# A streaming encoder layer: first normalisation in three steps, its transposed tiles through HBM by token tiles, and a right operand in four tiles

## Chip, cores and metric

The kernel runs on one core of a Trainium2 chip. Its matmuls run on TensorE (PE, whose weight loads PEld overlap them), elementwise work on VectorE (DVE), ScalarE (ACT) and GpSimd (POOL), and its DMAs are issued by SyncE (SP). The metric is the device time of one execution in microseconds (us), smaller is better; the median of three runs is given with their lowest and highest.

## What is computed

One layer over 2048 tokens of width 1024. The part before the output projection gives y (pooling and chunked attention over one input projection); what the change touches comes behind it:

```python
y = jnp.einsum('bse,ed->bsd', jnp.concatenate([y_pool, y_attn], axis=-1), w_out[l])
x = layer_norm(ALPHA * x + (1.0 + g1) * y, ln1_g[l], ln1_b[l])
h = x * (1.0 + sc2) + sh2
f = jnp.square(jax.nn.relu(jnp.einsum('bsd,df->bsf', h, w_ff1[l])))     # d_ff = 4096
f = jnp.einsum('bsf,fd->bsd', f, w_ff2[l])
x = layer_norm(ALPHA * x + (1.0 + g2) * f, ln2_g[l], ln2_b[l])
```

Inputs and output are float32. The kernel keeps that precision by cutting each operand into a rounded high part and a low remainder; a product is then three matmuls (high by high, high by low, low by high). Cutting (`split`) is a copy on ACT that rounds (CAST, L58) and a subtraction on DVE (L59).

## The kernel before

The program is one straight list of instructions for each engine, in the order in which the code is written; each engine takes its own list in order and waits on semaphores.

**Stages.** Attention and input projection run to about 640 us. Then comes the output projection with the first normalisation, to 873.8 us. FF1 follows to about 1532 us, and FF2 with the second normalisation ends the kernel.

**Output projection.** The 2048 tokens are 16 tiles of 128, t = 0 to 15. For each tile `st.get(yi[t])` gives the left operand: y is loaded from HBM (`raw<-yS`, L73) and cut into `hl`. The right operand, the weight `w_out`, cut, stands in one SBUF tile `hT` of 64 KB a partition. Each tile has two halves n of 24 matmuls (`wout_half`, L382), each into one of three PSUM banks `d`. `residual(t, n)` (DVE, L835) adds the bank to the tile of x, `xt`, and so frees it. After both halves `ln1_head` takes the statistics (DVE L773 and L775, three small POOL instructions) and writes the normalised tile `n` (ACT, L779). Tiles 0 to 2 are computed while the attention ends; the loop that matters runs over t = 3 to 15.

**From a normalised tile to FF1's operand.** `ln1_tail(u)` transposes a normalised tile u (8 PE transposes, L799, into one of two double-width PSUM tiles, T and S), scales it on ACT (8 instructions, L802) into `h`, and goes on by where the tile stands. Write b for the token half (tiles 0 to 7 and 8 to 15) and r = u mod 8. FF1 multiplies by seven combinations of quarter blocks (a Strassen scheme, pieces i = 0 to 6). For r < 4 two of the pieces are h itself. For r of 4 or more the tile's partner r − 4 comes back from HBM (`hp<-hS`, L796, two DMAs) and four DVE subtractions (`sums`, L820 to L823) make the other five. Pieces 0, 1, 2, 5 of token half 0 are cut into SBUF slots `sa` at once; the rest goes to HBM (`hS<-...`, L812). The tail of tile u stands between the two `residual` calls of a later tile t (u = t − 3 up to t = 6, where a second tail fits in, then u = t − 2). The last two tails come after the loop's body and behind the first products of FF1.

**FF1.** 32 groups g of output columns, seven products s each of 12 matmuls (L960): `f<-h,hl`, piece by weight combination. Results leave PSUM through an ACT copy `c` (L967) and DVE additions into tiles `g` (L973), are put through relu and square on ACT (L982, L983), combined, and stored (`fS<-g`, L1001). Pieces 3, 4 and 6 of token half 0 are loaded from `hS` in FF1's first group and cut there. The next group's weight is loaded, combined (`w_sums`, stored as `wS`) and cut (`w_split`) while a group runs.

**Order around the change.** All DMAs go through SP's one queue in program order. What a DMA waits for holds back all behind it. The buffers are few: two for `xt`, two for `raw`, three for `hl`, three for `n`, one each for `h` and `hp`.

Of the kernel before, what the change touches and what calls it, by code (L numbers as in the profile page):

```python
# [24 lines left out]
def trunk_layer(ctx: ExitStack, tc: tile.TileContext, xT, x, wada1, wada2, vecs, rows, win, wfirst, wpT, wout,  # L25
# [13 lines left out]
    hS = [[dram.tile([128, 4, 512], F32, name=f"hS{b}{i}") for i in range(7)] for b in range(2)]  # L39
# [74 lines left out]
    late = {}  # L114
    yi = [st.add(yS[t // 8][t % 8].rearrange("p k c -> p (k c)"), nc.vector) for t in range(16)]
    bigp = tc.tile_pool(name="big", bufs=1, side="right")
    big = bigp.__enter__()
    hT = big.tile([128, 2, 8, 1024], F32R, name="hT", tag="big")
# [42 lines left out]
    def dense0(k):  # L161
        for i, (a, b) in enumerate(((0, 0), (1, 0), (0, 1))):
            for c in range(NF0):
                for tb in range(2):
                    nc.tensor.matmul(first[c, tb], wf[:, a, k, c, :], hT[:, b, k, tb * 512:tb * 512 + 512],
                                     start=(k == 0 and i == 0), stop=(k == 7 and i == 2))
# [14 lines left out]
    def fold0(k):  # L181
# [6 lines left out]
        nc.scalar.activation(hT[:, 0, k, :], xk, AF.Identity, bias=mod1[:, k, 0:1], scale=mod1[:, k, 1:2])  # L188
        nc.scalar.activation(xk, xk, AF.Identity, bias=mod1[:, k, 0:1], scale=mod1[:, k, 1:2])

    def low0(k):
        wr, wa, xk = ld[k]
        nc.vector.tensor_sub(hT[:, 1, k, :], xk, hT[:, 0, k, :].bitcast(F32))
# [59 lines left out]
    def h_pieces(tb):  # L253
# [10 lines left out]
        for k in range(10):  # L264
# [131 lines left out]
    def dense():  # L396
        w, open_, side = {}, [], iter(())
        for hf, name, tb in blocks():
# [264 lines left out]
    def wo_pieces(n):  # L663
# [78 lines left out]
    def slot(i, name):  # L742

        pool, tag, n = (sap, "sa", 4) if i in (0, 1, 2, 5) else (late["sbp"], "sb", 3)
        return pool.tile([128, 2, 4, 512], F32R, name=name, tag=tag, bufs=n)

    cpool = tc.tile_pool(name="cp", bufs=1)
    cp = cpool.__enter__()
    lnp = tc.tile_pool(name="ln", bufs=1)
# [39 lines left out]
    def ln1_tail(t):  # L789
        b, r = t // 8, t % 8  # L790
        cols = slice((r % 4) * 128, (r % 4) * 128 + 128)
# [5 lines left out]
        pt = wide("S" if t % 2 and t < 15 else "T")  # L797
# [560 lines left out]
```

## Time and profile before

| what | value |
|---|---|
| median of 3 runs (lowest, highest) | 2167.26 us (2165.09, 2168.88) |
| the profiled execution: time, span of its trace | 2166.34 us, 2164.6 us |
| PE busy | 2059.5 us, 95% of the span |
| DVE, ACT, POOL busy | 61%, 46%, 20% |
| mean granted TensorE clock | 0.983 |
| output projection loop and FF1's first 18 products, 689.02 to 941.90 us | PE busy 222.80 of 252.88 us, clock 0.93 |
| FF1's middle, 1000 to 1500 us | PE busy 493.07 of 500 us, clock 0.99 |

The profiled execution was 1.74 us longer than its span, and 0.92 us under the median. A row of the trace gives the start, the busy time, the engine, the line of the code, the operation with its tiles as out<-in, and in brackets how long the engine was idle before it and what released it. A busy time of PE with a clock below 1.00 contains matmuls that ran at the lower of TensorE's two clocks.

### The profile page before, as it was taken

What the parts mean: (1) busy time and instruction counts of PE and PEld (TensorE: products, weight loads), DVE (VectorE), ACT (ScalarE), POOL (GpSimd) and SP (SyncE); (2) the same over time, 40 slices, a digit from 0 to 9 for tenths busy, and PEclk for the clock granted to TensorE, in tenths of its full rate; (3) what the DMA queues carried; (4) which work ended last, traced back from release to release, by engine and by line L of the source; (5) the groups of instructions that cost most, each with busy time, mean ns of one, the idle gap of its engine ahead of it and who ended that gap; (6) DMA issues with size and microseconds to landing.
All of it is one profiled execution on the core that took longest, in us unless ns stands there. A gap on an engine that the chain in (4) does not pass through costs nothing. (4 is left out here: it accounts for less than half of the span.)

```text
span 2164.6 us, 27212 instructions
## 1 busy us (share of the span) xinstructions
PE 2059.5 (95%) x9672; PEld 1696.2 (78%) x9672; DVE 1319.5 (61%) x1930; ACT 997.6 (46%) x1596; POOL 427.8 (20%) x474
## 2 busy tenths in 40 slices
PE   7999989999999988799999899999999999989997
PEld 6778878888887866578888688888778888878886
DVE  7555555556664453577766665666586448974448
ACT  4454555555553543445555655455444333243331
POOL 1535454553242000000000000000170004510002
PEclk9999999999999999899999999999999999999999
DMA  7444553444443666888787888887866556675552
GB/s 292 143 130 121 152 156 92 124 136 123 137 127 103 192 194 204 265 280 307 274 294 276 294 299 291 292 300 278 314 236 236 191 189 230 221 246 195 194 185 107
DMA packets 236457, 455.64 MB, mean 211 GB/s; under 512 B 19105, under 2 KB 69793, under 8 KB 234786
## 3 DMA queue, kind: packets, MB, share of 16 engines
q1 hardware_dynamic: 236322, 453.91, 62.8%
q8 instruction: 76, 1.25, 0.2%
q14 instruction: 59, 0.48, 0.1%
HBM read 294.45 MB, written 151.00 MB: 206 GB/s over the span
## 5 line engine op out<-in xcount | busy, mean ns | idle before, releaser
L960 PE MATMUL f<-h,hl 128*128 128x512 f32 x2688 | 627.4, 395 | 19.9 <-DVE h L59 7.5
L1246 PE MATMUL f<-sb,sa 128*128 128x512 f32 x2688 | 619.8, 393 | 10.2 <-DVE sb L59 9.6
L960 PEld LDWEIGHTS f<-h,hl 128*128 128x128 f32 x2688 | 508.9, 190 | 138.8 <-DVE h L59 8.6
L1246 PEld LDWEIGHTS f<-sb,sa 128*128 128x128 f32 x2688 | 506.6, 189 | 123.3 <-DVE sb L59 11.7
L418 PE MATMUL d<-hT,hl 128*128 128x512 f32 x1392 | 374.6, 401 | 1.9 <-ACT vt L313 1.9
L418 PEld LDWEIGHTS d<-hT,hl 128*128 128x128 f32 x1392 | 250.1, 190 | 42.5 <-ACT vt L313 2.3
L632 DVE TENSOR_TENSOR PT<-T,PT 128x640 fp32r<-128x640 f32 (+4 forms) x128 | 94.8, 741 | 218.4 <-ACT PT L631 216.4
L609 ACT ACTIVATE s<-s,m 128x640 f32<-128x640 f32 (+4 forms) x128 | 97.8, 764 | 222.0 <-DVE m L607 171.0
L382 PE MATMUL d<-hT,hl 128*128 128x512 f32 x696 | 174.7, 409 | 9.6 <-DVE xt L835 9.6
L382 PEld LDWEIGHTS d<-hT,hl 128*128 128x128 f32 x696 | 134.9, 197 | 39.7 <-issue 10.8
L982 ACT ACTIVATE g<-g 128x512 f32<-128x512 f32 x96 | 60.8, 633 | 212.6 <-DVE g L973 205.3
L59 DVE TENSOR_TENSOR sb<-hl,sb 128x1024 fp32r<-128x1024 f32 x67 | 96.6, 1442 | 84.4 <-ACT sb L58 83.8
L58 ACT CAST sb<-hl 128x1024 fp32r<-128x1024 f32 x67 | 70.1, 1046 | 163.0 <-PE f L1246 142.6
L615 POOL TENSOR_SCALAR s<-s,m 128x640 f32<-128x640 f32 (+4 forms) x128 | 96.6, 755 | 242.1 <-DVE m L614 199.7
L1287 POOL TENSOR_SCALAR ag<-ag 128x1024 f32<-128x1024 f32 x1 | 1.3, 1340 | 680.7 <-DMA ag<-in_rows_dram 680.7
L59 DVE TENSOR_TENSOR hl<-wsum,hl 128x1024 fp32r<-128x1024 f32 x62 | 75.9, 1225 | 92.1 <-ACT hl L58 92.1
L59 DVE TENSOR_TENSOR sb<-raw,sb 128x1024 fp32r<-128x1024 f32 x45 | 70.1, 1557 | 63.2 <-ACT sb L58 62.9
L1215 POOL TENSOR_SCALAR zv<-zv 128x1 f32<-128x1 f32 x16 | 18.4, 1149 | 448.2 <-DVE zv L1214 448.2
L600 PE MATMUL S<-k,q 128*128 128x320 f32 (+1 forms) x448 | 92.0, 321 | 12.8 <-DVE m L607 12.8
L623 PE MATMUL T<-ident,s 128*128 128x128 f32 x560 | 83.9, 277 | 18.0 <-DVE PT L632 13.2
L623 PEld LDWEIGHTS T<-ident,s 128*128 128x128 f32 x560 | 67.3, 142 | 41.8 <-POOL hl L59 13.6
L58 ACT CAST sb<-raw 128x1024 fp32r<-128x1024 f32 x45 | 47.1, 1046 | 114.5 <-PE f L1246 92.1
(172 smaller groups left out, 2626.0 us busy)
## 6 DMA issues: line engine op xcount, KB each, us to landing
fS<-g SPq DMA_DIRECT2D x224, 256.0 KB, 3.6
hl<-fS SPq DMA_DIRECT2D x67, 512.0 KB, 4.9
hl<-tS SPq DMA_DIRECT2D x67, 512.0 KB, 5.0
w<-in_w_dram SPq DMA_DIRECT2D x46, 512.0 KB, 4.1
raw<-fS SPq DMA_DIRECT2D x45, 512.0 KB, 4.8
raw<-tS SPq DMA_DIRECT2D x45, 512.0 KB, 4.9
raw<-in_w_dram SPq DMA_DIRECT2D x34, 512.0 KB, 5.3
tS<-tw SPq DMA_DIRECT2D x64, 256.0 KB, 4.5
```

The lines of the kernel that those rows point to most:

```text
L58: nc.scalar.copy(hl_h, src)
L59: low.tensor_sub(hl_l, src, hl_h.bitcast(F32))
L382: nc.tensor.matmul(ps, yc[:, a, k, :], hT[:, b, k, cols], start=(k == 0 and i == 0), stop=(k == 7 and i == 2))
L418: nc.tensor.matmul(ps, w[name][:, a, k, :], hT[:, b, k, tb * 512:tb * 512 + 512], start=(n == 0), stop=(n == 23))
L600: nc.tensor.matmul(S[:, 512 * p:512 * p + wp], q[:, i * 128:i * 128 + 128], k[:, a, k0 + p * wp:k0 + p * wp + wp], start=(a == 0), stop=(a ...
L609: nc.scalar.activation(s[:, 0:w], s[:, 0:w], AF.Exp, bias=m[:, 0:1], scale=-1.0, accum_out=m[:, 1:2])
L615: nc.gpsimd.tensor_scalar(s[:, 0:nk * 128], s[:, 0:nk * 128], m[:, 1:2], 1.0, op0=ALU.mult, op1=ALU.mult)
L623: nc.tensor.transpose(t[:, j * 128:j * 128 + 128], s[:, j * 128:j * 128 + 128], ident)
L632: nc.vector.tensor_sub(ol, src, oh.bitcast(F32))
L960: nc.tensor.matmul(ps, w[:, p, c:c + 128], h[:, q, k, :], start=first and k == 0 and (p, q) == (0, 0), stop=k == 3 and p == 1, skip_group_ ...
L982: nc.scalar.activation(o, o, AF.Relu)
L1246: nc.tensor.matmul(bank, f, w, start=start, stop=stop, skip_group_check=True)
```

## The change

`ln1_tail` becomes three functions. `ln1_load(u)` fetches the partner tile, `ln1_turn(u)` stores the normalised tile to `xS` (now ahead of the transposes) and transposes and scales it, and `ln1_sums(u)` makes the pieces. They are called half a tile apart: behind the matmuls of a half of tile t come its residual, then the sums of the tile that was turned one half earlier, then the next turn; the statistics of tile t close it. The table `TURNS` says which tile is turned when: u = t − 3 for t = 3 to 10, two tiles each at t = 11 and 12, one each at 13 and 14, tile 14 between two halves of tile 15's contraction, and tile 15 after the third product of FF1.

Turned tiles `h` and `hp` now take turns in buffers `w` that FF1's weights use later. They go to HBM as whole token tiles `hP` (rows of 4 KB for each partition, where `hS` had rows of 512 bytes), so that the partner comes back in one DMA of 512 KB in place of two of 256 KB, and the stores are delayed by `after(12)`. The right operand `hT` is four tiles of two blocks of the contraction each; tile 15 is computed contraction half by contraction half over two banks, so that the first two of the four are free half a tile before its end. Slots `sb` and the tiles `g` live there afterwards, `gs` as one tile with a fixed ring of eight places. Pieces 3, 4 and 6 are loaded and cut (`op_load`, `op_split`) earlier, through `raw`.

```diff
-    def ln1_tail(t):
+    def ln1_load(t):
+        b, r = t // 8, t % 8
+        if r >= 4:
+            hps[t] = h_tile(t, "hp")
+            nc.sync.dma_start(hps[t], hP[b][0][r - 4])
+
+    def ln1_turn(t, bank="T"):
         n = n_tiles.pop(t)
-        if r >= 4:
-            hp = ln.tile([128, 8, 128], F32, name="hp")
-            for i in range(2):
-                nc.sync.dma_start(hp[:, 4 * i:4 * i + 4, :], hS[b][i][:, :, cols])
+        nc.sync.dma_start(xS[t // 8][(t % 8) * 128:(t % 8) * 128 + 128, :], n)
+        pt = wide(bank)
...
+    def ln1_sums(t, delay=12):
...
         if r < 4:
             put(0, lo)
             put(1, hi)
+            after(delay, lambda: nc.sync.dma_start(hP[b][0][r], h))
...
+            def store():
+                nc.sync.dma_start(hP[b][2][r - 4], hp)
+                nc.sync.dma_start(hP[b][1][r - 4], h)
+                if b:
+                    nc.sync.dma_start(h2S[r - 4], t2)
+            after(delay, store)
...
+    TURNS = {t: (t - 3,) if t < 11 else (2 * t - 14, 2 * t - 13) if t < 13 else (t - 1,) for t in range(3, 15)}
+    waiting = []
+    for t in range(3, 15):
...
+        if t == 13:
+            w_load(0, w_tiles())
+        if t == 14:
+            op_load(3)
         for n in range(2):
+            turn_now = len(TURNS[t]) == 2 or n == (t >= 13)
+            u = TURNS[t][n] if len(TURNS[t]) == 2 else TURNS[t][0]
+            if turn_now:
+                ln1_load(u)
             ps = dbank()
             for k in range(8):
                 run(wout_half(t, n, k, yc, ps))
             residual(t, n, ps)
+            if waiting:
+                ln1_sums(waiting.pop(0))
+            if turn_now:
+                ln1_turn(u, "S" if u % 2 else "T")
+                waiting.append(u)
+            if n and t == 14:
+                for i in range(2):
+                    w_sums(0, i, s_tile())
+            tick(6)
         ln1_head(t)
...
+    for kh in range(2):
+        for n in range(2):
+            for k in range(4 * kh, 4 * kh + 4):
+                run(wout_half(15, n, k, yc, ps[n]))
+        if kh == 0:
+            ln1_sums(waiting.pop(0))
+            ln1_turn(14)
+            late["sb"] = [big.tile([128, 2, 4, 512], F32R, name="sb", tag="big", bufs=4) for _ in range(2)]
+            op_split(3)
+            w_split(0, 1)
+        tick(6)
...
     def gtile():
-        return gp.tile([128, 512], F32, name="g", tag="g", bufs=8)
+        gturn[0] += 1
+        return gs[:, (gturn[0] - 1) % 8, :]
```

In the loop, DVE's list around tile 8 reads as follows before the change (L59 is the low part of y or of a piece, L835 a residual, L820 to L823 the sums, L773 and L775 the statistics).

```order
L59 TENSOR_TENSOR hl<-raw,hl 128x512 x2
L835 SCALAR_TENSOR_TENSOR xt<-xt,d 128x512
L820 TENSOR_TENSOR hp<-h,hp 128x512
L821 TENSOR_TENSOR t_7217<-h,hp 128x512
L822 TENSOR_TENSOR h<-h 128x512
L823 TENSOR_TENSOR hp<-hp,t_7217 128x512
L59 TENSOR_TENSOR h_7141<-t_7217,h_7141 128x4x128
L59 TENSOR_TENSOR h_7144<-h,h_7144 128x4x128
L835 SCALAR_TENSOR_TENSOR xt<-xt,d 128x512
L773 BN_STATS s_7257<-xt 128x6 x2
L775 BN_AGGR mv<-s_7257 128x2
```

After the change the same place on DVE has these rows (a tile `w` holds the partner, or h).

```order
L60 TENSOR_TENSOR hl<-raw,hl 128x512 x2
L872 SCALAR_TENSOR_TENSOR xt<-xt,d 128x512 x2
L854 TENSOR_TENSOR w<-w 128x512
L855 TENSOR_TENSOR c<-w 128x512
L856 TENSOR_TENSOR w<-w 128x512
L857 TENSOR_TENSOR w<-w,c 128x512
L60 TENSOR_TENSOR h_7207<-c,h_7207 128x4x128
L60 TENSOR_TENSOR h_7210<-w,h_7210 128x4x128
L779 BN_STATS s_7214<-xt 128x6 x2
L781 BN_AGGR mv<-s_7214 128x2
```

Both residuals now stand ahead of the sums, which still stand ahead of the statistics of the tile.

SP's list for one tile of the same stretch, before (xt is x's tile, xS the stored normalised tile, hS the pieces in HBM):

```order
L755 DMA xt_7266<-in_x_dram 128x1024
L73 DMA raw_7273<-yS1_66 128x1024
L796 DMA hp_7301<-hS00_81 128x4x128
L796 DMA hp_7301<-hS01_82 128x4x128
L812 DMA hS03_84<-hp_7301 512x1x128
L812 DMA hS04_85<-h_7313 512x1x128
L812 DMA hS06_87<-hp_7301 512x1x128
L830 DMA xS0_132<-n_7150 128x1024
```

And SP's list for one tile after the change (w_7333 is the partner of the tile that is about to be turned, w_7230 and w_7268 belong to the tile before):

```order
L761 DMA xt_7279<-in_x_dram 128x1024
L74 DMA raw_7331<-yS1_66 128x1024
L821 DMA w_7333<-hP00_81 128x1024
L825 DMA xS0_125<-n_7109 128x1024
L862 DMA hP02_83<-w_7230 128x1024
L863 DMA hP01_82<-w_7268 128x1024
```

The partner is one DMA where it was two, the store of n has moved ahead of the pieces' stores, and these are two DMAs of 512 KB where they were three of 256 KB, one tile later.

ACT's list from the scaling of tile 13 into the first products of FF1, before (L802 scales, L779 normalises, L58 casts, L967 is the copy of a product):

```order
L802 ACTIVATE h<-S,b_6607,a_6606 128x128 x8
L779 ACTIVATE n<-xt,mv 128x1024
L58 CAST hl<-raw 128x1024
L802 ACTIVATE h<-T,b_6607,a_6606 128x128 x8
L779 ACTIVATE n<-xt,mv 128x1024
L58 CAST hl<-ws_7878 128x1024
L967 COPY c<-f 128x512
L58 CAST hl<-ws_7881 128x1024
L802 ACTIVATE h<-T,b_6607,a_6606 128x128 x8
L58 CAST h_8091<-g 128x512 x4
L982 ACTIVATE g<-g 128x512
```

ACT at the same place after the change:

```order
L831 ACTIVATE w<-S,b_6606,a_6605 128x128 x8
L785 ACTIVATE n<-xt,mv 128x1024
L59 CAST hl<-w 128x1024
L831 ACTIVATE h<-T,b_6606,a_6605 128x128 x8
L59 CAST sb<-raw 128x2x4x128 x2
L59 CAST hl<-wsum 128x1024
L785 ACTIVATE n<-xt,mv 128x1024
L1048 COPY c<-f 128x512
L59 CAST hl<-wsum 128x1024
L59 CAST sb<-raw 128x2x4x128 x2
L831 ACTIVATE h<-T,b_6606,a_6605 128x128 x8
L1063 ACTIVATE g<-g 128x512
```

The casts of piece 3 (`sb<-raw`, the first pair) stand ahead of the last normalisation, those of piece 4 (the second pair) ahead of the scaling of tile 15 and of the first relu.

## Rows read from the trace of the kernel before

**Rows 1.** Busy time by stretch: PE, PEld, DVE, ACT, POOL, clock, DMA share, GB/s.

```profile
689.02:941.90 252.88, 222.80 (x969) 179.34 (x967) 126.01 (x196) 115.10 (x228) 15.05 (x45) 0.93 0.68 217
...
875.00:890.00 15.00, 9.06 (x41) 6.53 (x39) 4.98 (x8) 8.46 (x16) 1.00 (x3) 0.92 0.86 260
...
930.00:950.00 20.00, 18.39 (x80) 14.71 (x80) 17.05 (x21) 9.71 (x15) 0.00 (x0) 1.00 0.95 320
...
1000.00:1500.00 500.00, 493.07 (x2135) 402.77 (x2134) 333.35 (x422) 266.30 (x395) 0.00 (x0) 0.99 0.83 292
```

**Rows 2.** Timeline of PE in the loop where it waits for nothing.

```profile
707.19 11.25 PE L382 MATMUL d<-hT,hl 128*128 128x512 f32 x48
718.27 1.04 PE L799 MATMUL T<-ident,n 128*128 128x128 f32 x8
719.07 11.25 PE L382 MATMUL d<-hT,hl 128*128 128x512 f32 x48
```

**Rows 3.** Timeline of PE at its longer waits, loop and FF1's first group.

```profile
764.42 7.33 PE L382 MATMUL d<-hT,hl 128*128 128x512 f32 x24 [3.06 <-DVE xt L835]
...
845.21 1.09 PE L799 MATMUL S<-ident,n 128*128 128x128 f32 x8 [3.58 <-ACT n L779]
...
864.50 1.97 PE L799 MATMUL T<-ident,n 128*128 128x128 f32 x8 [5.60 <-ACT n L779]
...
891.78 5.06 PE L960 MATMUL f<-h,hl 128*128 128x512 f32 x11 [6.76 <-DVE h L59]
...
906.01 0.51 PE L960 MATMUL f<-h,hl 128*128 128x512 f32 x1 [2.63 <-ACT h L58]
907.27 34.63 PE L960 MATMUL f<-h,hl 128*128 128x512 f32 x143 [0.76 <-DVE h L59]
```

**Rows 4.** Timeline of all engines over one tile of the loop.

```profile
770.27 0.32 SPq L73 DMA_DIRECT2D raw<-yS  x1
770.69 1.25 SPq L796 DMA_DIRECT2D hp<-hS  x2
...
775.09 0.69 DVE L820 TENSOR_TENSOR hp<-h,hp 128x512 f32<-128x512 f32 x1 [4.25 <-issue]
...
778.90 0.68 DVE L835 SCALAR_TENSOR_TENSOR xt<-xt,d 128x512 f32<-128x512 f32 x1
779.50 1.28 DVE L773 BATCH_NORM_STATS2 s<-xt 128x6 f32<-128x512 f32 x2
...
782.47 1.25 ACT L779 ACTIVATE n<-xt,mv 128x1024 f32<-128x1024 f32 x1 [4.72 <-POOL mv L778]
...
784.25 1.29 DVE L59 TENSOR_TENSOR hl<-raw,hl 128x512 fp32r<-128x512 f32 x2 [3.16 <-ACT hl L58]
784.64 2.89 ACT L802 ACTIVATE h<-S,b,a 128x128 f32<-128x128 f32 x8
```

**Rows 5.** DMA issues from 735 to 800 us: count, KB each, median us to landing.

```profile
raw<-yS SPq DMA_DIRECT2D x4, 512.0 KB, 4.9
hp<-hS SPq DMA_DIRECT2D x8, 256.0 KB, 5.5
...
xt<-in_x_dram SPq DMA_DIRECT2D x3, 512.0 KB, 3.4
```

**Rows 6.** Timeline of ACT and DVE at the start of FF1.

```profile
879.64 0.57 ACT L967 COPY c<-f 128x512 f32<-128x512 f32 x1
...
880.11 1.05 ACT L58 CAST hl<-ws 128x1024 fp32r<-128x1024 f32 x1
...
881.20 1.23 DVE L59 TENSOR_TENSOR hl<-ws,hl 128x1024 fp32r<-128x1024 f32 x1 [0.20 <-ACT hl L58]
```

**Rows 7.** Timeline of DVE and SP between two groups of FF1.

```profile
1012.06 6.51 SPq L1001 DMA_DIRECT2D fS<-g x5
...
1018.75 0.68 DVE L973 TENSOR_TENSOR g<-f,c 128x512 f32<-128x512 f32 x1
```

**Rows 8.** DMAs of line 1001 (`fS<-g`), all 224 of them.

```profile
DMA to landing us min/median/max: 2.0/3.6/8.4
```

More of the change, by code (lines that the diff above doesn't have):

```diff
@@ L38, in trunk_layer @@
     gS = dram.tile([1, 1024], F32, name="gS")
-    hS = [[dram.tile([128, 4, 512], F32, name=f"hS{b}{i}") for i in range(7)] for b in range(2)]
+    hP = [[dram.tile([4, 128, 8, 128], F32, name=f"hP{b}{i}") for i in range(3)] for b in range(2)]
+    h2S = dram.tile([4, 128, 4, 128], F32, name="h2S")
     fS = [[dram.tile([16, 128, 512], F32, name=f"fS{b}{i}") for i in range(7)] for b in range(2)]
@@ L115, in trunk_layer, with hT @@
     yi = [st.add(yS[t // 8][t % 8].rearrange("p k c -> p (k c)"), nc.vector) for t in range(16)]
-    bigp = tc.tile_pool(name="big", bufs=1, side="right")
-    big = bigp.__enter__()
-    hT = big.tile([128, 2, 8, 1024], F32R, name="hT", tag="big")
+    big = ctx.enter_context(tc.tile_pool(name="big", bufs=1, side="right"))
+    hTs = [big.tile([128, 2, 2, 1024], F32R, name="hT", tag="big", bufs=4) for _ in range(4)]
+    def hT(a, k, cols=slice(0, 1024)):
+        return hTs[k // 2][:, a, k % 2, cols]
     e = small.tile([128, 8], F32, name="e")
@@ L840, in ln1_head @@
         if t + 2 < 16:
-            load_x(t + 2)
+            after(6 if t > 2 else 0, lambda: load_x(t + 2))
+            if t < 3:
+                flush()
     wraw, wsum, whl = {}, {}, {}
@@ L894, in trunk_layer @@
             residual(t, n, ps)
-            tail = ln1_tail(tails[t, n]) if (t, n) in tails else ()
-            for _ in tail:
-                if n:
-                    break
-        ln1_head(t)
-        run(tail)
-        tick(12)
-        if t == 13:
-            w_load(0, [stream.tile([128, 1024], F32, name="raw", tag="raw", bufs=2) for _ in range(2)])
-            for i in range(2):
-                w_sums(0, i, ln.tile([128, 1024], F32, name=f"ws{i}"))
-        if t >= 14:
-            w_split(0, t - 14)
-    flush()
-    bigp.__exit__(None, None, None)
-    late["sbp"] = ctx.enter_context(tc.tile_pool(name="sb", bufs=1, side="right"))
-    gpool = tc.tile_pool(name="g", bufs=1, side="right")
-    gp = gpool.__enter__()
+            if waiting:
[7 more added lines that the diff above has]
+            tick(6)
+        ln1_head(t)
+    yc = st.get(yi[15]).rearrange("p a (k c) -> p a k c", k=8)
+    ps = [dbank() for _ in range(2)]
+    ln1_load(14)
+    w_split(0, 0)
+    for kh in range(2):
[9 more added lines that the diff above has]
+        tick(6)
+    for n in range(2):
+        residual(15, n, ps[n])
+    ln1_head(15)
+    flush()
+    w_load(1, late["w"])
+    op_load(4)
+    ln1_sums(14, 1)
+    late["sb"].append(big.tile([128, 2, 4, 512], F32R, name="sb", tag="big", bufs=4))
+    gs, gturn = big.tile([128, 8, 512], F32, name="g", tag="big", bufs=4), [0]
     def gtile():
-        return gp.tile([128, 512], F32, name="g", tag="g", bufs=8)
+        gturn[0] += 1
+        return gs[:, (gturn[0] - 1) % 8, :]
     psR.__exit__(None, None, None)
@@ L1069, in refill @@
         for c in range(2):
-            split(hslot[i][:, 0, 2 * c:2 * c + 2], hslot[i][:, 1, 2 * c:2 * c + 2], parts[c],
-                  nc.vector)
+            op_put(i, c, parts[c])
     back, refills = [], []
-    def w_tiles():
-        return [ffp.tile([128, 1024], F32, name="w", bufs=4) for _ in range(2)]
-    def s_tile():
-        return ffp.tile([128, 1024], F32, name="wsum", bufs=2)
     f2_items = [(b, i, kq, c, kind) for b in range(2) for i in range(7) for kq in range(4) for c in range(2)
```

158 lines of the change are left out of this document (91 added, 67 removed).

## Prediction

> **What bounds the kernel now.** I read the busy shares by stretch first. In FF1's middle PE is busy 493 of 500 us [rows 1], so nothing is to be won there. The stretch that the change rewrites runs from tile 3 of the output projection to 941.90 us in FF1's third group: 252.88 us, of which PE is busy 222.80 at a mean clock of 0.93 [rows 1]. What would it take undisturbed? In the quiet part of the loop 48 matmuls and 8 transposes follow one another: the transposes take 719.07 − 718.27 = 0.80 us, and the matmuls (719.07 − 707.19 − 0.80) / 48 = 0.231 us each [rows 2]. The stretch holds 13 × 48 matmuls of the projection, 18 × 12 of FF1, and 16 × 8 transposes: 840 × 0.2308 + 16 × 0.80 = 206.7 us. So **46.2 us are lost**: 30.1 while PE idles, 16.1 because matmuls run at the lower of the two clocks and in small gaps.
>
> The PE timeline then shows where it idles. In the loop PE waits for a residual (3.06 us at 764.42, and twice more), because no PSUM bank is free. At the loop's end it waits for a normalised tile (3.58 and 5.60 us), and in FF1's first group for pieces 4 and 6 (6.76; then 2.63 and 0.76) [rows 3]. The all-engine timeline shows why the residual is late. DVE stands idle for 4.25 us until the partner tile has landed, makes the sums and two low parts (775.09 to 778.90), and only then comes the second residual [rows 4].
>
> **The loop.** The matmuls, casts and subtractions stay as many as they were, so the gain can only be in waits. Moving the sums behind both residuals frees PE's bank: the three residual waits go. But the sums still stand ahead of the tile's statistics, and the statistics head a ring: statistics, normalisation on ACT, cast and low part of y, which frees `raw`; SP then issues the next y and the next partner, whose landing the next sums wait for. With the rows of one tile:
> - y to partner issue: 770.69 − 770.27 = 0.42
> - partner issue to first sum, L: see below
> - sums and two low parts: 778.90 − 775.09 = 3.81
> - statistics to the end of y's low part: 784.25 + 1.29 − 779.50 = 6.04 [rows 4]
>
> The residual (0.60) leaves the ring, so it takes 10.27 + L. What is L? Today it is 775.09 − 770.69 = 4.40 in that tile [rows 4]; by medians the two small DMAs land after 5.5, y (512 KB, as the new one) after 4.9, x alone after 3.4 [rows 5]. One DMA of the same bytes in longer rows is not shown by any trace; I bound it by 3.4 and 5.5 and take 4.7, nearest to y's row and today's. The ring is then 15.0 us against PE's 48 × 0.231 + 0.80 = 11.9.
>
> It turns four times (partners for tiles 4 to 7, at t = 7 to 10). Count from the start of tile 7's matmuls: residual 0.60, two low parts at 3.81 / 6 each 1.27, and 6.04 make 7.9. Four tiles later y's low part ends 7.9 + 4 × 3.1 = 20.3 us behind the start of tile 11. The scaling of tile 8 ends 1.99 later (784.64 + 2.89 against 785.54 [rows 4]), at 22.3. It must have emptied PSUM tile T before tile 10 can be turned, which is due behind 72 matmuls and two turns, at 18.2. **Wait 1: 4.1 us** (none at L = 3.4; 7.3 at 5.5).
>
> The Trainium skill, page "DMA: Bandwidth & Descriptors", section Bandwidth, gives 6.15 us of transfer for 1 MB. Y and partner are 1 MB together; an estimate by that page is L = 5.7, wait 1 of 8.1, and a time of 2148. The trace has moved the same bytes faster: 4.8 us from y's issue to the first sum [rows 4], so I keep 4.7.
>
> **The end of the loop and FF1's first group.** Tile 14 is now turned between the contraction halves of tile 15. Behind (14, 1) DVE has a residual 0.60, four weight sums 2.54, and statistics to the end of the normalisation take 782.47 + 1.25 − 779.50 = 4.22 [rows 4]: 7.4. PE meanwhile has one turn and 24 matmuls, 6.3. **Wait 2: 1.0.** The 3.58 and 5.60 go.
>
> FF1's third product needs the PSUM bank of its first, whose copy stands on ACT behind the normalisation of tile 15, and this behind the scaling of tile 14, the casts of piece 3 and of a weight sum. From the end of turn 14: 0.3 + 2.89 [rows 4], three casts at 1.05, a low part 1.23 [rows 6], two residuals 1.2, 4.22, and the copy 0.57 [rows 6] make 13.6, against 48 matmuls, 11.1. **Wait 3: 2.5.** Then the copy for the fifth product stands behind a weight cast, two casts of piece 4, the scaling of tile 15, two relu steps and another cast: about 8.4, against 24 matmuls and a turn, 6.3; that is 2.1 if piece 4 has landed, and 3.4 more if it is as late as piece 6 is today (2.63 + 0.76 [rows 3]). **Wait 4: 3.8**, the middle. **Wait 5**, piece 6: between nothing and today's 3.4; I take 2.4, nearer to today, as its load is still queued behind weights. Products 1 to 3 no longer meet the 6.76.
>
> **The sum.** 4.1 + 1.0 + 2.5 + 3.8 + 2.4 = 13.8 us of waits. Today 30.1 us of waits come with 16.1 of slow matmuls; in proportion 13.8 bring 7.4. Lost: 21.2 in place of 46.2, a gain of 25.0. From the profiled execution's 2166.34 that leaves 2141.3; it lies 0.92 under the median, so I say **2142 us**. With each wait at its bounds (0, 1.0, 2.5, 2.1, 0 to 7.3, 1.0, 2.5, 5.5, 3.4, times 1.53) it is 2129 to 2151.
>
> Costed at nothing: the stores in rows of 4 KB (off every path as long as SP is not behind), the earlier xS store (it lets the normalised tile's buffer go sooner, where nothing waits on PE's side), the finer waits on `sb` in FF2, and the reordered stores at group 31.
>
> **Rivals.**
> - *Late transfers in FF1's first group.* Pieces 3, 4 and 6, a weight of 1 MB, and the delayed stores are all queued within some 40 us. From 875 to 890 the DMAs moved 260 GB/s at a share of 0.86; the fullest stretch shows 320 at 0.95 [rows 1]. If pieces 4 and 6 land 6 to 13 us later than I reckon, waits 4 and 5 grow by as much: 2142 + 9 to 20 makes 2151 to 2162. For it: today's 6.76 stands here. Against: piece 3 no longer meets a wait at all.
> - *The ring is shorter.* L at 3.4 and group 0 clean: 2126 to 2133. Against: y and partner are issued together, x alone.
> - *Slower, by the ring of eight `g` tiles.* The first addition of a group (s = 1) now writes the place whose store was issued when the group before was being finished. In the timeline that store goes at 1012.06 and the addition at 1018.75, 6.7 us later [rows 7]. Stores land after 3.6 as a median and 8.4 at most [rows 8]. Landings of 8.4 every time would hold DVE, and behind it PE's banks, for 1.7 us in 30 groups: 51, thus 2193. It decides against the change once they average 25 / 30 = 0.8 over 6.7, so 7.5 us. Against: the median is half of that.
> - *No change.* The waits of the loop come back in full as wait 1 and in group 0 (30 us in all). It would take L of 7.5 and the late transfers together: 2162 to 2171.
>
> **How the numbers follow.** Forecast (2133 to 2151) 0.53; late transfers 0.19; shorter ring 0.12; no change 0.05; slower 0.11. A measurement of this kernel can tell about 0.2%, 4.3 us. Faster 0.84, the same 0.05, slower 0.11. The range leaves out the slower case and the lowest part of the shorter ring: 2127 to 2163; the forecast's own is 2133 to 2151.
>
> **What would show it.** The rows on which PE waited for a residual are gone. DVE's first sum follows the partner's issue by about 4.7 us, four times, and those tiles are 15 us apart on DVE. PE waits about 4 us ahead of the turn of tile 10, and for three of FF1's first seven products, but not for its second. DVE's first addition in later groups does not wait for a store. The prediction is wrong if L leaves 3.4 to 5.5, if FF1's first group loses more than 15 us, or if FF1 from group 2 on is longer than before.

## The result and the profile after

| | before | changed | ratio, 95% interval |
|---|---|---|---|
| first comparison (4 runs each) | 2168.07 us (2165.09 to 2170.88) | 2142.73 us (2141.10 to 2148.31) | 0.9893 [0.9873, 0.9914] |
| again, with the last experiments | 2167.11 us (2162.81 to 2169.53) | 2145.56 us (2144.13 to 2147.14) | 0.9904 [0.9891, 0.9918] |

The change makes the kernel about 1% faster. 2142 was predicted. The profiled execution of the first comparison took 2148.31 us, the longest of its four, with 249.07 us for the last 1055 matmuls of FF2 that took 243.13 in the profile of the second comparison, so the stretch that the change rewrites is the better measure. It runs from tile 3's first matmul to the end of FF1's 18th product ("the stretch" below). The busy times by stretch, which answer to [rows 1]:

```profile
688.59:918.84 230.25, 214.45 (x969) 175.08 (x967) 125.32 (x192) 114.25 (x224) 16.44 (x45) 0.97 0.69 243
1000.00:1500.00 500.00, 492.22 (x2127) 401.85 (x2126) 326.19 (x412) 266.97 (x394) 0.00 (x0) 0.99 0.81 285
```

The stretch takes 230.25 us in place of 252.88, 22.6 less; with the undisturbed 206.7, 23.6 are lost where it was 46.2. FF1's middle is as busy as before (492 against 493 of 500). PE's waits in the stretch, from its timeline, answer to [rows 3]:

```profile
794.27 7.38 PE L385 MATMUL d<-hT,hl 128*128 128x512 f32 x24 [4.11 <-DVE xt L872]
...
811.59 1.45 PE L828 MATMUL T<-ident,n 128*128 128x128 f32 x8 [3.54 <-ACT w L831]
...
850.99 1.09 PE L828 MATMUL T<-ident,n 128*128 128x128 f32 x8 [1.05 <-ACT n L785]
...
866.70 4.62 PE L1041 MATMUL f<-h,hl 128*128 128x512 f32 x12 [3.61 <-ACT c L1048]
...
877.41 4.41 PE L1041 MATMUL f<-sb,hl 128*128 128x512 f32 x12 [2.46 <-ACT c L1048]
...
885.62 3.00 PE L1041 MATMUL f<-sb,hl 128*128 128x512 f32 x12 [1.03 <-DVE g L1054]
```

They add up to 15.8 us (30.1 before). Two of them stand in the loop (a residual at 794.27, and the turn of tile 10, which waits for tile 8's scaling to empty T), one ahead of the turn of tile 14, three in FF1's first group. Where did the 22.6 us come from? I cut the stretch at two points: where PE begins to wait for a normalised tile at the loop's end (841.63 before, 849.94 after), and at FF1's first matmul. From each piece I take off its undisturbed time (0.2308 for a matmul, 0.80 for a turn):

| lost in | before | after | gain |
|---|---|---|---|
| the loop | 14.8 | 11.7 | 3.1 |
| from there to FF1's first matmul | 13.9 | 1.2 | 12.8 |
| FF1's products 1 to 18 | 17.5 | 10.7 | 6.7 |

So most of the gain does not come from the loop, and its 3.1 us are hardly more than the loop differs from one profile to the next: from tile 3 to FF1's first matmul pass 168.9 and 168.3 us in the two profiles of the changed kernel (184.7 before), and 166.1 to 168.3 in those of runs 3, 5, 6 and 8 below, which leave the loop as it is.

In FF1 the longest wait before, the 6.76 of [rows 3], is gone. The prediction put it down to piece 4. FF1's product s reads piece s, both counted from 0, so the fourth product, which waited, reads piece 3. Its low part stood on DVE behind the sums of tile 15, and these waited 6.03 us for their partner. In the kernel before:

```profile
888.45 0.69 DVE L820 TENSOR_TENSOR hp<-h,hp 128x512 f32<-128x512 f32 x1 [6.03 <-DMA hp<-hS]
...
891.04 2.49 DVE L59 TENSOR_TENSOR h<-g,h 128x512 fp32r<-128x512 f32 x4
```

After the change the low part of piece 3 is done at 858.41, and the fourth product (871.95) waits for nothing.

What the loop does now shows in the timeline of one tile, which answers to [rows 4] (DVE L854 is the first sum, L779 the statistics, L60 y's low part):

```profile
760.11 0.32 SPq L74 DMA_DIRECT2D raw<-yS  x1
760.47 0.43 SPq L821 DMA_DIRECT2D w<-hP  x1
760.95 0.43 SPq L825 DMA_DIRECT2D xS<-n  x1
761.47 0.38 SPq L862 DMA_DIRECT2D hP<-w  x1
761.89 0.55 SPq L863 DMA_DIRECT2D hP<-w  x1
762.48 1.50 SPq L761 DMA_DIRECT2D xt<-in_x_dram  x1
...
766.26 0.69 DVE L854 TENSOR_TENSOR w<-w 128x512 f32<-128x512 f32 x1 [4.99 <-DMA w<-hP]
...
770.08 1.28 DVE L779 BATCH_NORM_STATS2 s<-xt 128x6 f32<-128x512 f32 x2
...
774.84 1.30 DVE L60 TENSOR_TENSOR hl<-raw,hl 128x512 fp32r<-128x512 f32 x2 [3.17 <-ACT hl L59]
```

From the partner's issue (760.47) to the first sum (766.26) pass 5.79 us; in the four tiles 5.65, 5.79, 7.17 and 5.61, a mean of 6.06. The first sums stand at 750.21, 766.26, 783.75 and 799.68, 16.5 us apart on average: the ring is not shorter than before, when they were 16.1 apart. Behind the partner SP has put four more DMAs within 2.0 us, 2 MB in all. DMA issues from 740 to 800 us answer to [rows 5]:

```profile
hP<-w SPq DMA_DIRECT2D x7, 512.0 KB, 7.5
raw<-yS SPq DMA_DIRECT2D x4, 512.0 KB, 4.1
w<-hP SPq DMA_DIRECT2D x4, 512.0 KB, 5.7
xS<-n SPq DMA_DIRECT2D x4, 512.0 KB, 6.4
xt<-in_x_dram SPq DMA_DIRECT2D x4, 512.0 KB, 8.6
```

The load of x, which landed after 3.4 us when it was issued ahead of y [rows 5], now needs 8.6 as the last of this bunch.

### The profile page after: what moved, and what is told of

Read it like the earlier page. It is cut to its first block, busy times and chain, and to the rows that moved or that the text cites. A ratio compares the mean times of both kernels' runs of the same rounds, so it can differ in the third digit from the quotient of the medians.

```text
span 2146.5 us, 27078 instructions
## 1 busy us (share of the span) xinstructions
PE 2054.8 (96%) x9672; PEld 1691.9 (79%) x9672; DVE 1324.2 (62%) x1926; ACT 1002.8 (47%) x1592; POOL 429.5 (20%) x474
## 5 line engine op out<-in xcount | busy, mean ns | idle before, releaser
L421 PE MATMUL d<-hT,hl 128*128 128x512 f32 x1392 | 373.0, 400 | 1.9 <-ACT vt L316 1.9
L1041 PE MATMUL f<-h,hl 128*128 128x512 f32 x1536 | 364.6, 393 | 6.2 <-ACT c L1048 6.2
L1041 PEld LDWEIGHTS f<-h,hl 128*128 128x128 f32 x1536 | 289.8, 189 | 72.3 <-ACT c L1048 7.0
L1041 PE MATMUL f<-sb,hl 128*128 128x512 f32 x1152 | 281.6, 398 | 10.3 <-ACT c L1048 6.2
L421 PEld LDWEIGHTS d<-hT,hl 128*128 128x128 f32 x1392 | 248.9, 189 | 42.3 <-ACT vt L316 2.3
L1041 PEld LDWEIGHTS f<-sb,hl 128*128 128x128 f32 x1152 | 219.4, 191 | 61.5 <-ACT c L1048 7.5
L385 PE MATMUL d<-hT,hl 128*128 128x512 f32 x696 | 169.0, 400 | 4.1 <-DVE xt L872 4.1
L385 PEld LDWEIGHTS d<-hT,hl 128*128 128x128 f32 x696 | 131.5, 192 | 32.1 <-DVE xt L872 4.3
L59 ACT CAST sb<-hl 128x1024 fp32r<-128x1024 f32 x67 | 70.4, 1050 | 152.2 <-PE f L1322 128.8
L60 DVE TENSOR_TENSOR sb<-hl,sb 128x1024 fp32r<-128x1024 f32 x67 | 95.1, 1420 | 73.8 <-ACT sb L59 73.5
L60 DVE TENSOR_TENSOR hl<-wsum,hl 128x1024 fp32r<-128x1024 f32 x64 | 78.4, 1225 | 95.2 <-ACT hl L59 95.1
L60 DVE TENSOR_TENSOR sb<-raw,sb 128x1024 fp32r<-128x1024 f32 x55 | 84.6, 1544 | 54.7 <-ACT sb L59 54.5
L59 ACT CAST sb<-raw 128x1024 fp32r<-128x1024 f32 x55 | 57.4, 1051 | 114.1 <-PE f L1322 87.7
L60 DVE TENSOR_TENSOR hl<-w,hl 128x1024 fp32r<-128x1024 f32 x64 | 61.3, 958 | 70.0 <-ACT hl L59 70.0
```

Source lines behind the costliest of these rows:

```text
L59: nc.scalar.copy(hl_h, src)
L60: low.tensor_sub(hl_l, src, hl_h.bitcast(F32))
L385: nc.tensor.matmul(ps, yc[:, a, k, :], hT(b, k, cols), start=(k == 0 and i == 0), stop=(k == 7 and i == 2))
L421: nc.tensor.matmul(ps, w[name][:, a, k, :], hT(b, k, slice(tb * 512, tb * 512 + 512)), start=(n == 0), stop=(n == 23))
L1041: nc.tensor.matmul(ps, w[:, p, c:c + 128], h[:, q, k, :], start=first and k == 0 and (p, q) == (0, 0), stop=k == 3 and p == 1, skip_group_ ...
```

## The experiments

Twelve kernels ran. Times are medians of 4 to 10 runs, each with the ratio to the kernel before on the same chip and its interval; the stretch comes from each one's profile and shows where a difference lies (230.25 and 230.14 in the two profiles of the changed kernel). It is not good to tenths: the two loop waits, 7.65 and 7.19 us together in the changed kernel, make 5.3, 6.2, 8.1 and 6.7 in runs 3, 5, 6 and 8, which leave the loop as it is. So less than about 3 us in the loop cannot be told from nothing.

**1. Stores earlier.** The pieces' stores are issued right behind the sums.

```diff
-    def ln1_sums(t, delay=12):
+    def ln1_sums(t, delay=6):
```

> The stores of the pieces are issued right behind the sums (delay 6) and no longer behind the next partner load. Theory A (the delayed stores of 1 MB, issued 0.9 us behind the partner load, share the DMA engines with it): partner issue to first sum falls from a mean of 6.06 us to 4.4 to 4.9, the four tiles with a partner follow each other on DVE every 14.7 to 15.2 us in place of 16.5, PE's two loop waits of 4.11 and 3.54 shrink to 2 to 4 together, and the stretch from tile 3 to FF1's 18th product falls from 230.3 to 221 to 226 us: 4 to 9 us faster than the changed kernel, about 2135 us. Theory B (the landing is set by y and the partner themselves): 6.06 stays within 0.5, and so do the ring and the time, 2143 +- 3.

2141.1 us, 0.9893 [0.9877, 0.9909]; stretch 229.8. Partner issue to first sum: 5.54, 5.62, 5.89, 5.48, a mean of 5.63, 0.43 less than with the stores behind it, and the ring 15.9 in place of 16.5. The two loop waits are 2.50 and 4.96, together 7.46. Theory B holds by its own bound, and the sum of the waits hardly moves. Not all of the 0.43 is the stores': with the stores in place, runs 3, 5, 6, 8, 11 and 12 have means of 5.68 to 5.93 and rings of 16.0 to 16.2. What keeps the landing at 5.6 with the stores gone (y, partner, xS and x are still 2 MB within 1.4 us) was not taken apart further.

**2. Sums between the residuals again.**

```diff
-            residual(t, n, ps)
             if waiting:
                 ln1_sums(waiting.pop(0))
+            residual(t, n, ps)
```

> In the loop the sums stand again between the two residuals of a tile, as before the change; all else stays changed. Theory A (the gain in the loop comes from freeing PE's bank ahead of the sums): PE waits for a residual three or four times between 755 and 815 us, 3 to 5 us each, 10 to 16 us in all with their slow matmuls against 7.65 now, the stretch grows to 236 to 242 and the time to 2149 to 2155. Rival (the ring of 16.5 us sets the loop, wherever the residual stands): the lag of four tiles is the same, waits of 7 to 9 us in all, stretch 229 to 233, time as the changed kernel within 3 us.

2144.8 us, 0.9906 [0.9889, 0.9924]; stretch 231.4. The loop waits are 4.08, 1.71 and 2.19, together 7.98 in place of 7.65. The rival holds: with a ring of 16.5 us against 11.9 of matmuls, it does not matter much which instruction the lag is met at. My step "moving the sums behind both residuals frees PE's bank" is worth about 1 us here, which cannot be told from nothing.

**3. Tile 15 by column halves again.**

```diff
     for kh in range(2):
-        for n in range(2):
-            for k in range(4 * kh, 4 * kh + 4):
-                run(wout_half(15, n, k, yc, ps[n]))
+        for k in range(8):
+            run(wout_half(15, kh, k, yc, ps[kh]))
```

> Tile 15 is computed half by half over the columns again, not by contraction halves; tile 14 is still turned between the two. The first two parts of the right operand are then read until the tile's end, so slots for pieces 3 and 4 come free 5.5 us later. Theory A (this early freeing is what lets piece 3 be cut ahead of the last normalisation): the casts of piece 3 start about 857.5 in place of 854.9, hold back the last normalisation on ACT and DVE's residuals of tile 15, and the third product waits 6 to 7 us in place of 3.61; stretch 233 to 236, time 2146 to 2150. Rival (ACT has room): third product's wait within 0.7 of 3.61, time 2143 +- 3.

2144.2 us, 0.9908 [0.9888, 0.9928]; stretch 228.0 (its loop waits are 2.4 us less than in the changed kernel). The third product waits 3.63, as with 3.61. The rival holds: freeing half of the right operand early is worth nothing that can be measured.

**4. The kernel before, with only the sums moved behind both residuals** (a tail is taken in two steps).

```diff
+        yield
         lo, hi = h[:, 0:4], h[:, 4:8]
...
-            tail = ln1_tail(tails[t, n]) if (t, n) in tails else ()
-            for _ in tail:
-                if n:
-                    break
+            if n:
+                run(tail)
+                tail = ()
+            if (t, n) in tails:
+                tail = ln1_tail(tails[t, n])
+                for _ in range(1 + n):
+                    next(tail)
```

> The kernel before with one part of the change alone: in the loop the sums of a tile come behind both residuals of the next half pair (one tail in two steps), nothing else. Theory A (two gains that add up: residuals no longer behind sums in the loop, and the earlier work in FF1's first group): PE's three residual waits (9.6 us and their slow matmuls) go or fall to one, 5 to 10 us faster than before, 2158 to 2163; FF1's first group keeps its waits of 11.3 us. Rival (the order of the sums is worth nothing by itself, since the ring decides): 2168 +- 4, with waits for other releasers of 8 us or more in the loop.

2166.7 us, 1.0014 [1.0003, 1.0026]; stretch 253.7. PE's timeline:

```profile
768.00 11.27 PE L382 MATMUL d<-hT,hl 128*128 128x512 f32 x48 [1.34 <-DVE xt L836]
...
838.86 1.97 PE L799 MATMUL S<-ident,n 128*128 128x128 f32 x8 [3.58 <-ACT n L779]
...
857.64 1.97 PE L799 MATMUL T<-ident,n 128*128 128x128 f32 x8 [5.24 <-ACT n L779]
...
888.56 4.90 PE L964 MATMUL f<-h,hl 128*128 128x512 f32 x11 [8.41 <-DVE h L59]
...
904.26 0.80 PE L964 MATMUL f<-h,hl 128*128 128x512 f32 x1 [4.12 <-ACT h L58]
```

The loop's waits become six small ones of 0.7 to 1.4 us (the first row is one), after most of which the matmuls run at full speed. FF1 begins 179.3 us after tile 3 in place of 184.7: 5.5 us are won. They are all given back in FF1's first group, which waits 8.41 and 4.12 where it waited 6.76 and 2.63 [rows 3]: 74.5 us from FF1's first matmul to the 18th product's end, in place of 68.1. The 8.41 is again the low part of piece 3 behind the sums of tile 15, whose partner DVE now awaits for 7.67 us; the 4.12 is piece 6. Theory A had the loop's gain right (5.5 us, for 5 to 10) and the time wrong: a gain in the loop is worth nothing as long as that partner and piece 6 come late.

**5. Tile 15 turned one product later.**

```diff
-                elif s == 2:
-                    ln1_turn(15)
-                elif s == 3:
-                    ln1_sums(15, 1)
-                elif s == 4:
-                    op_split(6)
+                elif s == 3:
+                    ln1_turn(15)
+                elif s == 4:
+                    op_split(6)
+                    ln1_sums(15, 1)
```

> Tile 15 is turned behind FF1's fourth product in place of the third, and its sums come one product later; on ACT the copy for the fifth product then stands ahead of the scaling of tile 15. Theory A (that copy's place in ACT's list makes the fifth product's wait of 2.46 us): the wait goes, with its slow matmuls 3 to 4.5 us, time 2 to 5 us under the changed kernel's 2142.7; the stretch from tile 3 to FF1's 18th product falls from 230.3 to 226 to 227.5. Rival (piece 4's landing, or piece 6 behind it, sets the group): the fifth or seventh product waits as much, 2 to 3.5 us, and the time stays within 2 us.

2144.2 us, 0.9900 [0.9885, 0.9915]; stretch 231.2. The fifth product's wait is gone (its copy is now ahead of the scaling), and comes back at the sixth (0.70) and seventh:

```profile
886.05 4.98 PE L1041 MATMUL f<-sb,hl 128*128 128x512 f32 x12 [4.70 <-DVE g L1054]
```

The rival's time, but neither its wait (2 to 3.5 us) nor its cause: piece 6 was cut by 881.64; the seventh product waits for the addition that reads the fifth's result, which stands on DVE behind four sums and a low part.

**6. As 5, and the sums of tile 14 behind the weight's third part.**

```diff
     op_load(4)
-    ln1_sums(14, 1)
...
             if (g, s) == (0, 0):
                 w_split(0, 2)
+                ln1_sums(14, 0)
+                tick(0)
```

> As the run with tile 15 turned later, and the sums of tile 14 also move: on DVE behind the third weight part of FF1's first group, so that DVE is idle while POOL does the three small steps of tile 15's statistics. Theory A (those three steps took 0.47, 1.00 and 0.83 us in place of 0.19, 0.55 and 0.27, since DVE ran two-operand instructions at the same time): they take 0.19, 0.55 and 0.27 again, and the third product's wait falls from 3.61 to 2.2 to 2.6; 1 to 2 us more gain. Rival (POOL's slowness has another cause): 1.00 stays, and so does the 3.61.

2147.6 us, 0.9917 [0.9902, 0.9932]; stretch 233.6. The three POOL steps of tile 15's statistics, in the changed kernel:

```profile
862.42 0.47 POOL L782 TENSOR_SCALAR mv<-mv 128x1 f32<-128x1 f32 x1 [12.75 <-DVE mv L781]
862.97 1.00 POOL L783 TENSOR_TENSOR mv<-mv,mhalf 128x1 f32<-128x1 f32 x1
864.07 0.83 POOL L784 TENSOR_SCALAR mv<-mv 128x1 f32<-128x1 f32 x1
```

and in this run, with DVE idle beside them:

```profile
861.14 0.19 POOL L782 TENSOR_SCALAR mv<-mv 128x1 f32<-128x1 f32 x1 [12.74 <-DVE mv L781]
861.41 0.55 POOL L783 TENSOR_TENSOR mv<-mv,mhalf 128x1 f32<-128x1 f32 x1
862.06 0.27 POOL L784 TENSOR_SCALAR mv<-mv 128x1 f32<-128x1 f32 x1
```

The third product's wait falls from 3.61 to 2.31. Theory A holds for the mechanism. The time is worse all the same: with the sums moved into the first group its fifth product waits 3.27 and its seventh 6.15.

**7. Partner loaded ahead of y** (with the stores as in 1).

```diff
     for t in range(3, 15):
+        if t < 11:
+            ln1_load(TURNS[t][0])
         yc = st.get(yi[t]).rearrange("p a (k c) -> p a k c", k=8)
...
-            if turn_now:
+            if turn_now and t > 10:
                 ln1_load(u)
```

> The partner of the tile to be turned next is loaded ahead of y in SP's list, right behind the stores of the sums, which are issued half a tile earlier as in the first run. The partner's landing then lies beside the rest of the ring. Theory A (the ring of 16 us, with the partner's 5.5 to 6 us in it, makes both loop waits): tiles with a partner follow each other on DVE every 11.9 to 12.3 us, DVE's first sum does not wait for the partner, PE's waits of 4.11 and 3.54 go, the stretch falls from 230.3 to 217 to 221, the time to 2130 to 2134. Rival (what the loop gains is given back in FF1's first group, as in the kernel before with its sums late): the loop ends 9 to 12 us earlier, but the waits in FF1's first group grow from 7.1 to 14 us or more, and the time stays above 2139.

2132.4 us, 0.9850 [0.9832, 0.9868]; stretch 219.5. DVE's first sums no longer wait, and keep PE's step:

```profile
749.96 0.68 DVE L854 TENSOR_TENSOR w<-w 128x512 f32<-128x512 f32 x1
...
761.84 0.68 DVE L854 TENSOR_TENSOR w<-w 128x512 f32<-128x512 f32 x1
...
773.72 0.69 DVE L854 TENSOR_TENSOR w<-w 128x512 f32<-128x512 f32 x1
...
785.59 0.68 DVE L854 TENSOR_TENSOR w<-w 128x512 f32<-128x512 f32 x1
```

They are 11.88 us apart, and both loop waits are gone. FF1 begins 157.5 us after tile 3 (168.9 in the changed kernel), and its first 18 products take 62.0 in place of 61.4: nothing is given back. Theory A holds in all its numbers. This kernel is faster than both the kernel before and the changed one.

**8. Piece 3 loaded behind the projection again** (and piece 4 after it).

```diff
-        if t == 14:
-            op_load(3)
...
-            op_split(3)
             w_split(0, 1)
...
-    op_load(4)
+    op_load(3)
     ln1_sums(14, 1)
...
+                if s == 0:
+                    op_split(3)
+                    op_load(4)
```

> Piece 3 is loaded behind the output projection, as in the kernel before, and cut behind FF1's first product; piece 4 follows it through the same two buffers. Theory A (a good part of the gain is that piece 3, and with it piece 4, comes early): FF1's fourth product waits 2 to 5 us and the fifth 4 to 8, waits in FF1's first group 12 us or more in place of 7.1, stretch 237 to 243, time 2150 to 2156. Rival (the two pieces had room): group waits within 2 us of 7.1, the third product's wait smaller by about 2, as the casts of piece 3 no longer stand ahead of the last normalisation, time 2139 to 2144.

2147.4 us, 0.9920 [0.9903, 0.9937]; stretch 234.7.

```profile
868.82 5.49 PE L1038 MATMUL f<-h,hl 128*128 128x512 f32 x12 [7.34 <-ACT c L1045]
...
881.19 4.62 PE L1038 MATMUL f<-sb,hl 128*128 128x512 f32 x12 [3.08 <-ACT c L1045]
```

The wait stands at the third product, 7.34 in place of 3.61, and not at the fourth, where I had it: ACT takes the casts of piece 3 in order, so the copy c stands behind casts that wait for a load. The loss is 4.4 us of stretch, under theory A's 7 to 13; FF1's first 18 products alone take 67.4 us in place of 61.4, 6.0 more, while the loop, which the edit leaves alone, happened to be 1.5 us shorter. Early loading matters, and through ACT's list.

**9. As 7, with the first group rearranged** (turn of tile 15 as in 5; its sums and the next weight's low part behind the addition).

```diff
-                elif s == 2:
+                elif s == 3:
                     ln1_turn(15)
-                elif s == 3:
-                    ln1_sums(15, 1)
                 elif s == 4:
                     op_split(6)
...
-                if s == 4:
+                if s == 4 and g:
                     w_split(g + 1, 0)
...
+            if (g, s) == (0, 4):
+                w_split(1, 0)
+                ln1_sums(15, 1)
```

> As the run with the partner loaded ahead, and in FF1's first group: tile 15 turned behind the fourth product (as in the fifth run), its sums and the next weight's first low part behind the addition of the fifth product's result, where they had stood ahead of it. Theory A (in the fifth run the fifth product's wait went, but the seventh then waited 4.70 us, because that addition stood on DVE behind the four sums and the low part): the fifth product's 2.45 goes and the seventh's wait is 2 us or less; waits in the group 4.5 to 6.5 in place of 6.9, time 2128 to 2131. Rival (the last products wait for piece 6 itself): the seventh waits 3 us or more, time 2131 to 2135.

2131.3 us, 0.9847 [0.9827, 0.9867]; stretch 221.5. The first group's waits are 3.64, 0.71 and 1.03, together 5.4 (6.9), as theory A had it. But the second group, which had none over 0.3, now waits 1.76 and 2.49: given back. Its time cannot be told from run 7's.

**10. Only the partner ahead, stores late as in the change** (7 without 1).

> Only the partner's load moves ahead of y; the pieces' stores stay delayed as in the change. Theory A (the ring held the landing, and the place of the stores matters only while it does): as the run that also moved the stores, PE waits for nothing from tile 3 to tile 14, time 2130 to 2134. Rival (the delayed stores slow the early partner load and y too): first sums wait for the partner again, 1 to 3 us per tile, and the loop keeps a wait of 2 to 4 us, time 2135 to 2139.

2132.6 us, 0.9847 [0.9830, 0.9864]; stretch 219.2, no wait in the loop, first sums 11.88 apart. Theory A holds: once the partner is out of the ring, the place of the stores is worth nothing that can be measured (2132.4 us and 219.5 in run 7).

**11. The changed kernel again**, beside 9 and 10.

> The changed kernel again, beside the last two on the same chip: 2141 to 2145, ratio to before 0.988 to 0.991. In its last 250 us (FF2's second half) the matmuls took 0.236 us on average in the first profile, 1.9% more than in the kernel before; if that belongs to the change it stands here too, if it belongs to that execution it does not.

2145.6 us, 0.6 above what I expected; loop waits 3.57 and 3.62, stretch 230.1; FF2's last 1055 matmuls 243.13 us.

**12. Tiles 12 and 13 turned half a tile earlier** (for tile 13 this is its place before the change; tile 12 was turned behind the second half of tile 13 there too).

```diff
-            turn_now = len(TURNS[t]) == 2 or n == (t >= 13)
+            turn_now = len(TURNS[t]) == 2 or n == 0
...
         if kh == 0:
-            ln1_sums(waiting.pop(0))
             ln1_turn(14)
```

> Tiles 12 and 13 are turned behind the first half of tiles 13 and 14, as in the kernel before, and no longer behind the second; their sums move half a tile with them, and so stand ahead of the statistics of tiles 13 and 14. All else as changed. Theory A (the gain between the loop and FF1 comes from half a tile more between a tile's statistics and its turn): tile 13's turn waits 1.5 to 2.5 us and tile 14's 4 to 4.6 in place of 0 and 1.05 (residual 0.6, sums 2.5, weight sums 2.5 and 4.2 to the normalised tile, against 5.5 of matmuls), the stretch grows from 230.2 to 236 to 239, the time to 2149 to 2153. Rival (the waits before came from the loads in that place, not from the place of the turn): neither turn waits over 1.5 us, time within 3 us of the changed kernel.

2150.2 us, 0.9935 [0.9913, 0.9958]; stretch 237.0.

```profile
839.90 1.09 PE L828 MATMUL S<-ident,n 128*128 128x128 f32 x8 [2.01 <-ACT n L785]
...
856.54 1.90 PE L828 MATMUL T<-ident,n 128*128 128x128 f32 x8 [4.54 <-ACT n L785]
```

Both turns wait, as theory A had them: 6.55 us, where 3.58 and 5.60 [rows 3] made 9.18. Reckoned as in the table above, 8.5 us are lost between the loop and FF1, against 1.2 in the changed kernel and 13.9 before. So the places of the turns and sums make more than half of the middle part of the gain: a turn behind the second half leaves PE 48 matmuls beside the statistics and the normalisation, and the sums of a tile stand ahead of no statistics that PE will soon wait for. The edit moves turns and sums together, so their shares are not shown. The rest, some 5 us, was not tested. The trace of the kernel before has a rival for it: DVE stood idle until FF1's first weight had landed, with both residuals and the statistics of tile 14 behind it in its list.

```profile
853.90 0.69 DVE L860 TENSOR_TENSOR ws<-raw 128x512 f32<-128x512 f32 x1 [11.37 <-DMA raw<-in_w_dram]
```

The changed kernel issues that load at 823.61 us in place of 846.05, and its weight sums wait for nothing.

## Why the prediction was right, step by step

The time came out at 2142.7 and 2145.6 for 2142. The mechanism held in outline: a ring that is longer than PE's step makes waits in the loop, and ACT's and DVE's lists make those in FF1's first group. But four of the five waits were off by 1 us or more, two too small and two too large, so that the sum is right in part by luck. By two of its own signs the prediction was wrong: L left its bounds, and a residual still makes PE wait.

- **L, and wait 1.** 4.7 was taken within 3.4 to 5.5; the mean is 6.06 in the first profile of the changed kernel, and 5.7 to 5.9 in six more with the same loop (runs 3, 5, 6, 8, 11 and 12). "Today's" 4.40 was read from one tile. The trace of the kernel before has four, and these are the other three:

```profile
738.45 1.98 SPq L796 DMA_DIRECT2D hp<-hS  x2
...
743.89 0.69 DVE L820 TENSOR_TENSOR hp<-h,hp 128x512 f32<-128x512 f32 x1 [4.33 <-DMA hp<-hS]
...
754.20 1.53 SPq L796 DMA_DIRECT2D hp<-hS  x2
...
759.78 0.69 DVE L820 TENSOR_TENSOR hp<-h,hp 128x512 f32<-128x512 f32 x1 [5.44 <-issue]
...
786.00 1.25 SPq L796 DMA_DIRECT2D hp<-hS  x2
...
792.25 0.69 DVE L820 TENSOR_TENSOR hp<-h,hp 128x512 f32<-128x512 f32 x1 [6.11 <-issue]
```

  They make 5.44, 5.58 and 6.25 us; with the 4.40, the shortest, the mean is 5.42. With 5.42 the prediction's own count gives a wait 1 of 4.1 + 4 × 0.72 = 7.0. Measured are 4.11 + 3.54 = 7.65, over half of it at a residual that I had not seen as a place where the lag is met. With 6.06 the count makes the turn of tile 10 9.5 us late; it was due at 801.8 (tile 11 starts at 783.58) and came at 811.59, 9.8 late, 7.65 of it as waits and most of the rest in the slower matmuls between them. So the ring was counted rightly, and its L was mis-sized. That the ring with the landing in it makes these waits is shown by runs 7 and 10. Why L is 0.3 to 0.6 us longer than before was not taken apart. The change puts xS, two stores and x (2 MB) behind the partner, and I had costed the stores at nothing, but taking the two stores away (run 1) gives 5.63, hardly less than the 5.68 to 5.93 of the same loop with them. Whether one DMA in longer rows lands sooner than two, no run shows. The estimate that the prediction made from the Trainium skill's page "DMA: Bandwidth & Descriptors", section Bandwidth, whose figure is of transfers that GpSimd issues, was an L of 5.7, so with 5.7 to 6.1 measured the page was nearer here than the row that I preferred.
- **Wait 2** was 1.05 for 1.0.
- **Wait 3** was 3.61 for 2.5: 1.3 of it is POOL's slowness beside DVE's sums (run 6).
- **Wait 4** was 2.46 for 3.8. Piece 4 had landed; only ACT's list counts, near the 2.1 that I gave for that case.
- **Wait 5** was 1.03 for 2.4, and not for piece 6, but for an addition on DVE.
- **The sum.** Waits 15.8 for 13.8, slow matmuls and gaps 7.8 for 7.4: lost 23.6 for 21.2, a gain of 22.6 for 25.0 in the stretch. The medians of the first comparison lie 25.3 apart and those of the second 21.6; both agree with 22.6 within their intervals, so that the first lies within 1 us of 2142 is luck.
- **Late transfers in FF1's first group** did not come: pieces 4 and 6 were there in time. The 6.76 that was counted for this rival was piece 3's low part behind the sums of tile 15 on DVE, as shown above. From FF1's 19th product on FF1 took 580.1 us before, and 582.0 and 580.5 in the two profiles of the changed kernel; the other runs lie between 579.2 and 581.4, so no loss is shown there.
- **The ring of eight `g` tiles** did not bite. Stores land as before (answering to [rows 8]), and the addition still comes some 6.7 us behind the store's issue, without a wait for it. In all of FF1 one DVE instruction waited for such a store, for 0.2 us.

```profile
DMA to landing us min/median/max: 2.0/3.6/8.8
```

```profile
988.96 6.22 SPq L1082 DMA_DIRECT2D fS<-g  x5
```

```profile
995.64 0.69 DVE L1054 TENSOR_TENSOR g<-f,c 128x512 f32<-128x512 f32 x1 [0.20 <-DVE g L1073]
```

- **Which part earns what.** Half a tile more between statistics and turn at the loop's end, with the sums moved along: 6.7 us of stretch when undone for tiles 12 and 13 (run 12). Pieces 3 and 4 early: 4.4 of stretch, 6.0 in FF1 alone (run 8). Sums behind both residuals: not to be told from nothing (run 2). Tile 15 by contraction halves: nothing (run 3). About half of the 22.6 remains; the turns in pairs and the earlier load of the first weight are among it, and it was not taken apart.

## What to carry to other kernels

A prefetch that stands in a queue behind a load that waits for a buffer is no prefetch: the changed kernel issues the partner's load 7.6 us behind the last of the sums before it, run 10 2.1 us behind, and moving that one line was worth about 10 us, nearly half of what the whole change brought. A gain in one stage counts only if the next stage's inputs come earlier too (run 4). In runs 5, 6 and 9 a wait that was removed by reordering an in-order engine reappeared at a later reader; none of the three came out clearly ahead. When a prediction takes a landing from the old trace, read it from every tile of the stretch and not from one, and count what is issued around the transfer that somebody waits for.

## What the runs showed of the hardware

POOL's three small steps took 0.19, 0.55 and 0.27 us in every tile of the loop; in the last tile, beside DVE's subtractions of two SBUF tiles, 0.47, 1.00 and 0.83, and again 0.19, 0.55 and 0.27 when these were moved (run 6). It is not any work on DVE that slows them: for tile 2 of the changed kernel they ran beside a residual, which reads one tile from SBUF and one from PSUM, and beside the statistics, which read one tile from SBUF, and kept their time to 0.02 us.

```profile
687.20 0.63 DVE L872 SCALAR_TENSOR_TENSOR xt<-xt,S 128x512 f32<-128x512 f32 x1
687.37 0.19 POOL L782 TENSOR_SCALAR mv<-mv 128x1 f32<-128x1 f32 x1 [10.76 <-DVE mv L781]
687.65 0.57 POOL L783 TENSOR_TENSOR mv<-mv,mhalf 128x1 f32<-128x1 f32 x1
687.75 1.28 DVE L779 BATCH_NORM_STATS2 s<-xt 128x6 f32<-128x512 f32 x2
688.32 0.27 POOL L784 TENSOR_SCALAR mv<-mv 128x1 f32<-128x1 f32 x1
```

The Trainium skill states on the page "SBUF — State Buffer", section "Who interferes with whom", that a DVE instruction with two SBUF inputs contends with a GpSimd instruction that reads SBUF; the trace agrees, and gives the price.

What a wait costs in clock is not to be told from its length alone. After 2.50 us (run 1), 2.81 (run 12) and 3.03 us (run 6) at the same place of the loop the next 24 matmuls took 5.79, 5.79 and 5.78 us at a granted clock of 1.00, as in a quiet stretch; after 2.69 (run 5), 3.02 (run 8) and 4.11 us (the changed kernel) they took 7.37, 7.10 and 7.38 at a mean granted clock of 0.76, 0.79 and 0.77, part of them at the lower of TensorE's two clocks.
